# Two feature tiles of a feed-forward block by pairs of token tiles, with a new order of its first stage, on one Trainium2 core

## The chip, the cores and the metric

The kernel runs on one core of a Trainium2 chip. The metric is the device time of one execution in microseconds (us). Three runs of the kernel before took 2253.65, 2257.54 and 2258.06 us; the median is 2257.54 us. TensorE is the matmul engine (PE in the profile, PEld its weight loads), VectorE is DVE, ScalarE is ACT, GpSimd is POOL, and SyncE (SP) issues the DMAs. Each engine works through its own queue in order; an instruction that waits holds up what stands behind it on the same engine.

## The reference

Two layers of an encoder are applied to 512 prompt tokens and 256 sample tokens with the same weights (768 tokens, width 1024). A layer has four mixers side by side (grouped-query attention, differential attention, retention, RWKV-7) and then a gated feed-forward block of width 2816:

```python
mix = jnp.concatenate([o_a, o_b, o_c, o_d], axis=-1) @ p['w_out'][l]
x = x + _rms(mix, p['norm_mix_post'][l])
h = _rms(x, p['norm_ffn_pre'][l])
f = (jax.nn.silu(h @ p['ffn_w_gate'][l]) * (h @ p['ffn_w_up'][l])) @ p['ffn_w_down'][l]
x = x + _rms(f, p['norm_ffn_post'][l])
```

`_rms` scales a row by `rsqrt(mean(x*x) + eps)` and by a gain. All is float32.

## The kernel before

Each float32 operand of a matmul is split into a high part (a copy that ScalarE rounds) and a low part (the difference, by VectorE or GpSimd), and a product is three matmuls: high by high, high by low, low by high. The normalised activations stand transposed in `hh` and `hl`, eight rows of 128 features by 768 tokens; the tokens are six tiles of 128, tiles 0 to 3 of the prompt (sequence 0) and 4 and 5 of the sample (sequence 1).

The order of the instructions of the mixers, and of the start of the feed-forward block, is set by a planner that simulates the queues and gives earlier program text priority. Under `manual_schedule` the order is that of the program text. This holds from `ffn_head` (L1346) to the end of the block.

**The end of the mixers.** `out` (L1167) adds the last products, applies `post_norm` (L226) and `pre_norm` (L218) per token tile, and `split_T` (L201) transposes each normalised tile on TensorE (tile name `hT`) and writes `hh` and `hl`. Each norm calls `rsqrt` (L149): a tensor_scalar (multiply and add, L153, VectorE) and a power of -1/2 (L154, GpSimd). `rsqrt` is called at six places: two kinds of norm of whole rows (names `p`, `q`, and `q_`, `p_` at the block's end), the head norms of attention and retention (`ra`, `rb`, `rc`) and the group norm (`fr`).

**The feed-forward block.** The 22 feature tiles of 128 are worked off in order. Tiles 2 to 21 use a block product with seven instead of eight half-size products (`block_mm`, L1262, tile name `p`), which needs sums of blocks of the activations (`ffn_sums`, L1207) and of the weights (`w_sums`, L1325). The first two, f = 0 and f = 1, are plain products (`up_mm`, L1275, by `feat_mm`, L189; tile names `fg` for the gate and `fu` for the up weight): for each sequence, and for each pair of token tiles in it, 24 matmuls for `fg` and 24 for `fu`. While TensorE works on them, the other engines make the sums. `up_gate` (L1284) turns `fg` and `fu` into the gated activation: tanh (ScalarE, L1288), two products (VectorE, L1289 and L1290), the high part `ah` (ScalarE, L1291) and the low part `al` (VectorE, L1292).

The down products (`down_mm`, L1294, tile name `dn`) multiply the gated activations of two feature tiles by the down weights for one token tile and one half of the outputs: six matmuls each, twelve of them for f = 0 and 1. They use two PSUM banks in turn, and `down_add` (L1307) empties a bank: for this first group ScalarE copies it (L1310), for later ones VectorE adds it (L1312).

**The head, written by hand.** `ffn` (L1614) makes the products and the gate of f = 0 for sequence 0 under the planner. `ffn_head` then has, in this order: products of f = 0 for sequence 1; both parts of sums 0 (`next(sums[0])` twice: first the adds of L1218 and the differences L1219 and L1220 on GpSimd, then the differences L1228 and L1229 and the splits L1232 and L1233); the two splits of down weights; the gate of f = 0, sequence 1; sums 1, with the products of f = 1 for sequence 0 in the middle; the weight splits of f = 2 (`w_first`, `w_second`); both parts of sums 2; the gate of f = 1, sequence 0; the products of f = 1, sequence 1; the first part of sums 3; the weight sums of f = 2; the gate of f = 1, sequence 1; two down products; the second part of sums 3; four splits (`ffn_first`); two down products; `w_third`. The remaining eight down products stand in the units of f = 2 and f = 3 of `ffn_units` (L1390), four in each; later units have six.

PSUM has eight banks. The products of sequence 0 use the tag `pS` (two banks: one for `fg`, one for `fu`), those of sequence 1 the tag `pb` (two banks), the down products `pa` (two), and the transposes `pT` and `pO` (one each).

Of the kernel before, what the change touches and what calls it, by code (L numbers as in the profile page):

```python
# [14 lines left out]
ALU = mybir.AluOpType  # L15
# [11 lines left out]
NT = TOK // P  # L27
# [58 lines left out]
class Trunk:  # L86
# [62 lines left out]
    def rsqrt(self, src, n, scale, eps, name, tag):  # L149

        nc = self.nc
        r = self.tiny(tag, n, name, 4)
        nc.vector.tensor_scalar(out=r, in0=src, scalar1=scale, scalar2=eps, op0=ALU.mult, op1=ALU.add)  # L153
        nc.gpsimd.tensor_tensor(out=r, in0=r, in1=self.mhalf.to_broadcast([P, n]), op=ALU.pow)  # L154
        return r

# [1118 lines left out]
    def up_mm(self, l, f, s, wg, wu):  # L1275

        t0, n, *_r = SEQS[s]
        pg, pu = [self.bank(("pS", "pb")[s], f"{n}{l}_{f}_{s}") for n in ("fg", "fu")]
        for a in range(0, n, 256):
            self.feat_mm(pg[:, a:a + 256], *wg, P, t0 + a, 256)  # L1280
            self.feat_mm(pu[:, a:a + 256], *wu, P, t0 + a, 256)
        return pg, pu

    def up_gate(self, s, pg, pu, th, ah, al):  # L1284
        nc = self.nc
# [60 lines left out]
    def ffn_head(self, l, ws, tiles):  # L1346

        self.raw, self.w, self.tt, self.t1s = {}, {}, {}, []
        A, V = self.nc.gpsimd, self.nc.vector
        self.nbank = 0  # L1350
        sums = [self.ffn_sums(l, k) for k in range(4)]
        act = [t[1:] for t in tiles]
        self.rest = [(t, n) for n in range(2) for t in range(NT)]

        def down(n):
            for _i in range(n):
                t, half = self.rest.pop(0)
                self.down_add(*self.down_mm(l, 0, t, half, (act, self.w["d", 0, half])))

        self.down_load(l, 0, 0)  # L1360
        self.down_load(l, 0, 1)
        ps = self.up_mm(l, 0, 1, *ws[0])
        next(sums[0])
        next(sums[0])
        self.down_split(l, 0, 0, eng=V)
        self.w_load(l, 2, 0)
        self.down_split(l, 0, 1, eng=A)
        self.w_load(l, 2, 1)
        self.up_gate(1, *ps, *tiles[0])
        next(sums[1])  # L1370
        ps = self.up_mm(l, 1, 0, *ws[1])
        next(sums[1])
        self.w_first(l, 2, ("whi", "wlo"))
        self.w_second(l, 2)
        next(sums[2])
        next(sums[2])
        self.up_gate(0, *ps, *tiles[1])
        ps = self.up_mm(l, 1, 1, *ws[1])
        next(sums[3])
        self.w_sums(2)  # L1380
        self.up_gate(1, *ps, *tiles[1])
        down(2)
        next(sums[3])
        for k in range(4):
            self.ffn_first(k)
        down(2)
        self.w_third(l, 2)
        return act

    def ffn_units(self, l, act):  # L1390
# [3 lines left out]
        nc = self.nc  # L1394
# [5 lines left out]
        NG = NF // 2  # L1400
# [5 lines left out]
        for f in range(2, NF):  # L1406
            nxt = f + 1 if f + 1 < NF else None
            g, odd = f // 2, f % 2
            G, U = self.tmp(f"fg{l}_{f}"), self.tmp(f"fu{l}_{f}")
            c11, c12, c21, c22 = G[:, L], G[:, R], U[:, L], U[:, R]  # L1410
            downs = [] if g == NG - 1 else self.rest[4 * odd:4 * odd + 4] if g == 1 else [(t, odd) for t in range(NT)]

            def mm(n, key, j, h):
                return self.block_mm(f"p{n}{l}_{f}", w[f, key], j, h)
# [199 lines left out]
    def ffn(self, l):  # L1614
        if l + 1 < L:
            self.xd = [self.dr.tile([P, DM], F32, name=f"xd{l}_{t}") for t in range(NT)]

        tiles = [(self.tmp(f"th{l}_{f}"), self.slot("D", [P, TOK], f"ah{l}_{f}", F32R), self.slot("D", [P, TOK], f"al{l}_{f}", F32R)) for f in range(2)]
        ws = []
        for f in range(2):  # L1620
            ws.append([self.piece(l, PIECE_FF + 2 * f + i, tags=("Q", "Q") if f and i else ("whi", "wlo")) for i in range(2)])
            if f == 0:
                self.up_gate(0, *self.up_mm(l, 0, 0, *ws[0]), *tiles[0])
        with self.tc.manual_schedule():
            act = self.ffn_head(l, ws, tiles)
            self.late = self.ffn_end(l, self.ffn_units(l, act))
# [184 lines left out]
```

## Time and profile before

| what | value |
|---|---|
| median of three runs | 2257.54 us (2253.65 to 2258.06) |
| the profiled execution | 2247.12 us |
| its span, first to last instruction | 2245.3 us |
| granted TensorE clock, mean share of full speed | 0.984 |
| TensorE busy | 2111.9 us (94%) |
| VectorE busy | 1599.2 us (71%) |
| ScalarE busy | 917.5 us (41%) |
| GpSimd busy | 909.3 us (40%) |

The durations come from the profiled execution. Its span starts with the first and ends with the last instruction; 1.8 us of its time lie around the span. Its time is 10.4 us under the median of the runs. A row of the timeline has the start, the duration, the engine, the line, the operation, output and inputs, the shape and the count; in brackets stands the idle time of the engine before it and what ended that. Matmuls are pipelined, so the distance from start to start is what one costs TensorE, not its duration.

### The profile page before, as it was taken

The page shows a single profiled execution, that of the slowest core. Times are in us where ns is not written, and L with a number is a line of the kernel's source. Part 1 is how long each engine was busy: PE and PEld are TensorE (multiplying, and loading weights), DVE is VectorE, ACT ScalarE, POOL GpSimd, SP SyncE. Part 2 cuts the span into 40 slices and gives each one's busy share as a digit, 9 for nine tenths or more (in the row PEclk, how much of TensorE's full clock was granted, in tenths as well). Part 3 has the DMA queues.
Part 4 walks back from the last instruction along what each step waited for, and adds up shares of the span by engine and source line. Part 5 has one row for each costly group of instructions (what it writes and reads, how often), then busy time and mean ns, then how long its engine had stood idle before and what let it go on. Part 6 is the DMA issues. An engine that isn't in the chain of part 4 may idle for free.

```text
span 2245.3 us, 43651 instructions
## 1 busy us (share of the span) xinstructions
PE 2111.9 (94%) x17400; PEld 1923.2 (86%) x17400; DVE 1599.2 (71%) x2782; ACT 917.5 (41%) x1865; POOL 909.3 (40%) x733
## 2 busy tenths in 40 slices
PE   7989989989889999999999998899899899999998
PEld 7878878779879999999888898887788799999996
DVE  5597647885876767767766885588857676777665
ACT  4333325565534332333434333355654433232322
POOL 1342212334555445454523333133254545445454
PEclk9999989999999999999999999999999999999999
DMA  4544365344412221212425535733353112221223
GB/s 173 140 103 119 95 214 138 92 139 146 140 47 76 66 75 62 70 66 66 174 97 139 130 87 141 219 114 95 119 168 112 48 66 76 66 75 58 71 70 141
DMA packets 245099, 240.93 MB, mean 107 GB/s; under 512 B 138784, under 2 KB 191904, under 8 KB 244896
## 3 DMA queue, kind: packets, MB, share of 16 engines
q1 hardware_dynamic: 244896, 238.15, 34.8%
q8 instruction: 137, 2.24, 0.4%
q14 instruction: 66, 0.54, 0.1%
HBM read 183.03 MB, written 55.05 MB: 106 GB/s over the span
## 4 chain that ended last, share of the span: by engine, by line
PE 63%; DVE 17%; DMA 6%; POOL 4%; issue 4%; ACT 4%; SPq 1%; DVEq 0%; POOLq 0%; ACTq 0%
PE p L1271 23%; PE dn L1303 15%; PE dz L197 5%; DMA raw<-in_wp_dram 3%; PE op L186 3%; PE za L186 2%; PE zb L186 2%; DVE el L461 2%; DVE nper L463 2%; PE sd L174 1%; PE zv L186 1%; PE ob L174 1%; POOL wlo L168 1%; DVE wlo L168 1%; DVE xm L234 1%
## 5 line engine op out<-in xcount | busy, mean ns | idle before, releaser
L1259 POOL TENSOR_TENSOR wld<-raw,whd 128x1024 fp32r<-128x1024 f32 x42 | 108.6, 2585 | 360.2 <-ACT whd L1258 360.2
L1303 PE MATMUL dn<-whd,ah 128*128 128x512 f32 x528 | 210.9, 400 | 20.7 <-ACT ah L1291 18.0
L1303 PE MATMUL dn<-wld,ah 128*128 128x512 f32 x528 | 210.0, 398 | 1.5 <-POOL wld L1259 1.5
L1303 PE MATMUL dn<-whd,al 128*128 128x512 f32 x528 | 210.3, 398 | 0.0
L1312 DVE TENSOR_TENSOR y<-y,dn 128x512 f32<-128x512 f32 x216 | 147.3, 683 | 80.4 <-PE dn L1303 80.4
L168 POOL TENSOR_TENSOR wlo<-raw,whi 128x1024 fp32r<-128x1024 f32 (+1 forms) x46 | 108.4, 2356 | 181.0 <-ACT whi L165 163.6
L1271 PE MATMUL p<-ts,whb 128*128 128x384 f32 x560 | 144.7, 339 | 0.0
L1259 POOL TENSOR_TENSOR wla<-raw,wha 128x1024 fp32r<-128x1024 f32 x40 | 96.2, 2405 | 110.9 <-ACT wha L1258 110.9
L1398 DVE TENSOR_TENSOR fg<-fg,p 128x384 f32<-128x384 f32 x160 | 87.9, 549 | 63.0 <-PE p L1271 62.8
L1303 PEld LDWEIGHTS dn<-whd,ah 128*128 128x128 f32 x528 | 100.1, 190 | 37.3 <-ACT ah L1291 18.9
L1424 ACT ACTIVATE ft<-fg 128x384 f32<-128x384 f32 x80 | 42.0, 525 | 208.3 <-DVE fg L1398 208.3
L165 ACT ACTIVATE whi<-raw 128x1024 fp32r<-128x1024 f32 (+1 forms) x95 | 92.2, 971 | 83.9 <-DMA raw<-in_wp_dram 38.2
L1303 PEld LDWEIGHTS dn<-whd,al 128*128 128x128 f32 x528 | 99.9, 189 | 24.5 <-DVE al L1485 0.5
L1258 ACT ACTIVATE whb<-raw 128x1024 fp32r<-128x1024 f32 x40 | 42.5, 1062 | 189.8 <-POOL raw L1331 189.8
L1303 PEld LDWEIGHTS dn<-wld,ah 128*128 128x128 f32 x528 | 100.6, 191 | 17.8 <-POOL wld L1259 2.4
L186 PE MATMUL zc<-whi,hh 128*128 128x256 f32 x384 | 112.1, 294 | 2.7 <-ACT zc L794 2.3
L1428 DVE SCALAR_TENSOR_TENSOR fg<-ft,fg 128x384 f32<-128x384 f32 x80 | 85.6, 1070 | 40.4 <-ACT ft L1424 40.4
L186 PE MATMUL zc<-wlo,hh 128*128 128x256 f32 x384 | 109.8, 287 | 1.0 <-DVE wlo L168 1.0
L186 PE MATMUL zc<-whi,hl 128*128 128x256 f32 x384 | 109.6, 286 | 0.0
L1271 PEld LDWEIGHTS p<-ts,whb 128*128 128x128 f32 x560 | 102.5, 188 | 6.3
L1271 PE MATMUL p<-hl,whc 128*128 128x384 f32 x320 | 107.6, 336 | 0.0
L1271 PE MATMUL p<-hh,whc 128*128 128x384 f32 x320 | 107.5, 336 | 0.0
(463 smaller groups left out, 7201.7 us busy)
## 6 DMA issues: line engine op xcount, KB each, us to landing
raw<-in_wp_dram SPq DMA_DIRECT2D x184, 512.0 KB
raw<-in_wp_dram SPq DMA_DIRECT2D x38, 384.0 KB
kr<-kd SPq DMA_DIRECT2D x96, 64.0 KB
kr<-kd SPq DMA_DIRECT2D x48, 128.0 KB
x<-xm SPq DMA_DIRECT2D x24, 256.0 KB
xf<-x SPq DMA_DIRECT2D x12, 512.0 KB
gain<-in_bc_dram SPq DMA_DIRECT2D x8, 512.0 KB
bd<-sh SPq DMA_DIRECT2D x8, 512.0 KB
```

Source lines behind the costliest of these rows:

```text
L165: nc.scalar.activation(hi[:, :n], raw[:, :n], AF.Copy)
L168: eng.tensor_tensor(out=lo[:, :n], in0=raw[:, :n], in1=hi[:, :n].bitcast(F32), op=ALU.subtract)
L174: self.nc.tensor.matmul(ps[c], lhsT=lhsT[:, c], rhs=rhs, start=start, stop=stop)
L186: mm(ps, lhsT=a, rhs=b[:, c:c + ncol], start=i == 0, stop=i == tot - 1)
L197: mm(ps, lhsT=a, rhs=b, start=i == 0, stop=i == 3 * NK - 1)
L461: V.tensor_tensor(out=ev, in0=q[:, j + 1:32, j:j + 1].to_broadcast([96, m, j]), in1=q[:, j:j + 1, 0:j].to_broadcast([96, m, j]), op=ALU.mult)
L1259: eng.tensor_tensor(out=lo, in0=x, in1=hi.bitcast(F32), op=ALU.subtract)
L1271: self.nc.tensor.matmul(ps, lhsT=a, rhs=b, start=i == 0, stop=i == 11)
L1303: self.nc.tensor.matmul(ps, lhsT=a[p], rhs=b[q], start=i == 0, stop=i == 6 * len(pairs) - 1)
L1312: self.nc.vector.tensor_tensor(out=yt, in0=yt, in1=ps, op=ALU.add)
L1398: add = lambda o, x, y, op=ALU.add: V.tensor_tensor(out=o, in0=x, in1=y, op=op)
L1428: V.scalar_tensor_tensor(out=x, in0=th, scalar=1.0, in1=x, op0=ALU.add, op1=ALU.mult)
```

## The change

`rsqrt` runs its tensor_scalar on GpSimd. `up_mm` becomes a generator that yields after each pair of token tiles, and its banks go by feature tile (f = 0 has `pS`, f = 1 has `pb`) instead of by sequence. In `ffn`, both feature tiles make their products for token tiles 0 and 1 first, and then for tiles 2 and 3, each followed by its gate, all under the planner. In `ffn_head` the products of f = 1 for sequence 0 and their gate are gone, the weight splits of the down products stand before the second part of sums 0, gates, sums and weight splits have another order, and eight down products instead of four stand in the head, so that two instead of four are left for each of the units f = 2 and f = 3.

```diff
@@ rsqrt
-        nc.vector.tensor_scalar(out=r, in0=src, scalar1=scale, scalar2=eps, op0=ALU.mult, op1=ALU.add)
+        nc.gpsimd.tensor_scalar(out=r, in0=src, scalar1=scale, scalar2=eps, op0=ALU.mult, op1=ALU.add)
@@ up_mm
-        pg, pu = [self.bank(("pS", "pb")[s], f"{n}{l}_{f}_{s}") for n in ("fg", "fu")]
+        pg, pu = [self.bank(("pS", "pb")[f], f"{n}{l}_{f}_{s}") for n in ("fg", "fu")]
         for a in range(0, n, 256):
             self.feat_mm(pg[:, a:a + 256], *wg, P, t0 + a, 256)
             self.feat_mm(pu[:, a:a + 256], *wu, P, t0 + a, 256)
-        return pg, pu
+            yield pg, pu
@@ ffn_head
-        ps = self.up_mm(l, 0, 1, *ws[0])
-        next(sums[0])
+        ps = next(self.up_mm(l, 0, 1, *ws[0]))
         next(sums[0])
         self.down_split(l, 0, 0, eng=V)
         self.w_load(l, 2, 0)
         self.down_split(l, 0, 1, eng=A)
         self.w_load(l, 2, 1)
+        next(sums[0])
+        next(sums[1])
         self.up_gate(1, *ps, *tiles[0])
+        ps = next(self.up_mm(l, 1, 1, *ws[1]))
         next(sums[1])
-        ps = self.up_mm(l, 1, 0, *ws[1])
-        next(sums[1])
-        self.w_first(l, 2, ("whi", "wlo"))
         self.w_second(l, 2)
         next(sums[2])
+        self.w_first(l, 2, ("whi", "wlo"))
+        self.up_gate(1, *ps, *tiles[1])
+        down(2)
         next(sums[2])
-        self.up_gate(0, *ps, *tiles[1])
-        ps = self.up_mm(l, 1, 1, *ws[1])
+        down(2)
         next(sums[3])
         self.w_sums(2)
-        self.up_gate(1, *ps, *tiles[1])
         down(2)
         next(sums[3])
@@ ffn_units
-            downs = [] if g == NG - 1 else self.rest[4 * odd:4 * odd + 4] if g == 1 else [(t, odd) for t in range(NT)]
+            downs = [] if g == NG - 1 else self.rest[2 * odd:2 * odd + 2] if g == 1 else [(t, odd) for t in range(NT)]
@@ ffn
+        ups = []
         for f in range(2):
             ws.append([self.piece(l, PIECE_FF + 2 * f + i, tags=("Q", "Q") if f and i else ("whi", "wlo")) for i in range(2)])
-            if f == 0:
-                self.up_gate(0, *self.up_mm(l, 0, 0, *ws[0]), *tiles[0])
+            ups.append(self.up_mm(l, f, 0, *ws[f]))
+            next(ups[f])
+        for f in range(2):
+            self.up_gate(0, *next(ups[f]), *tiles[f])
```

## Rows read from the trace of the kernel before

**Rows 1.** Page, busy time (us), share of the span and instructions of each engine.
```profile
PE 2111.9 (94%) x17400; PEld 1923.2 (86%) x17400; DVE 1599.2 (71%) x2782; ACT 917.5 (41%) x1865; POOL 909.3 (40%) x733
```

**Rows 2.** Waits of TensorE: us in total, times, longest us.
```profile
PE dn L1303 <- ACT ah L1291: 18.0, 2, 9.0
...
PE fg L197 <- DVE hl L211: 2.7, 4, 1.1
PE hT L206 <- DVE hl L211: 2.6, 2, 2.4
```

**Rows 3.** Timeline of TensorE in the first layer's head.
```profile
627.52 0.27 PE L197 MATMUL fu<-hh,wlo 128*128 128x256 f32 x1
627.64 0.28 PE L197 MATMUL fg<-hh,whi 128*128 128x256 f32 x1
...
633.34 0.40 PE L1303 MATMUL dn<-whd,ah 128*128 128x512 f32 x1
...
633.81 0.40 PE L1303 MATMUL dn<-whd,al 128*128 128x512 f32 x1
643.25 0.80 PE L1303 MATMUL dn<-whd,ah 128*128 128x512 f32 x1 [9.05 <-ACT ah L1291]
```

**Rows 4.** Timeline of ScalarE in the same head.
```profile
638.17 1.53 ACT L1232 ACTIVATE ts<-t 128x384 fp32r<-128x384 f32 x3 [8.30 <-DVE t L1228]
639.61 0.58 ACT L1288 ACTIVATE th<-fg 128x512 f32<-128x512 f32 x1
642.57 0.63 ACT L1291 ACTIVATE ah<-th 128x512 fp32r<-128x512 f32 x1 [2.38 <-DVE th L1290]
...
646.08 0.58 ACT L1310 ACTIVATE y<-dn 128x512 f32<-128x512 f32 x1
```

**Rows 5.** Timeline of VectorE in the same head.
```profile
629.57 3.23 DVE L1218 TENSOR_TENSOR t<-hh,hl 128x384 f32<-128x384 f32 x2
636.81 1.33 DVE L1228 TENSOR_TENSOR t<-t,t 128x384 f32<-128x384 f32 x1 [4.00 <-POOL t L1220]
...
643.84 1.02 DVE L1218 TENSOR_TENSOR t<-hh,hl 128x384 f32<-128x384 f32 x2
```

**Rows 6.** Timeline of GpSimd in the same head.
```profile
629.95 2.44 POOL L1259 TENSOR_TENSOR wla<-raw,wha 128x1024 fp32r<-128x1024 f32 x1 [3.70 <-ACT wha L1258]
...
635.78 0.99 POOL L1220 TENSOR_TENSOR t<-t,t 128x384 f32<-128x384 f32 x1
```

**Rows 7.** The chain that ended last, two pieces: start us, us, what.
```profile
643.25 7.77 PE dn L1303 x21
...
1755.24 6.59 PE dn L1303 x21
```

**Rows 8.** Stretches: us, then busy us of PE, PEld, DVE, ACT, POOL, clock, DMA share, GB/s.
```profile
580.00:611.00 31.00, 26.98 (x208) 25.58 (x207) 29.55 (x40) 16.12 (x28) 15.37 (x12) 0.94 0.37 121
611.00:634.00 23.00, 23.00 (x192) 22.72 (x191) 17.77 (x23) 6.98 (x12) 14.30 (x11) 1.00 0.15 47
```

**Rows 9.** Timeline of TensorE before the second layer's head.
```profile
1708.57 0.66 PE L206 MATMUL hT<-cs,xn 128*128 128x128 f32 x4 [2.40 <-DVE hl L211]
...
1711.31 0.58 PE L197 MATMUL fg<-hl,whi 128*128 128x256 f32 x1 [1.12 <-DVE hl L211]
```

**Rows 10.** First layer, second weight split of f = 4, and the product that reads it.
```profile
690.50 1.27 DVE L1259 TENSOR_TENSOR wlb<-raw,whb 128x1024 fp32r<-128x1024 f32 x1
...
699.11 0.52 PE L1271 MATMUL p<-ts,whb 128*128 128x384 f32 x2
```

**Rows 11.** Lines L153 and L154: duration ns min/median/max, first and last start us, forms.
```profile
L153 DVE TENSOR_SCALAR p5r<-p x3: 145/151/154, 11.1 to 1713.1; 128x1 f32<-128x1 f32 x3
...
L154 POOL TENSOR_TENSOR p5r<-p5r,mhalf x3: 548/549/553, 11.4 to 1713.4; 128x1 f32<-128x1 f32 x3
```

**Rows 12.** Groups of GpSimd by form: busy us, mean ns, idle before and its releaser.
```profile
L168 POOL TENSOR_TENSOR wlo<-raw,whi 128x1024 fp32r<-128x1024 f32 x26 | 68.7, 2644 | 136.2 <-ACT whi L165 118.8 <-PE sb L987 9.6 <-DMA nper<-nb 7.8
...
L553 POOL MEMSET br<- 64x128 f32 x96 | 19.1, 199 | 102.6 <-issue 31.0 <-ACT pb L756 24.9 <-ACT vb L794 10.7
```

## The prediction

> **What bounds the kernel now.** I read the busy times of the engines first: TensorE is busy for 94% of the span, so it sets the pace, and only what leaves it idle or slow can be won [rows 1]. The list of TensorE's waits says where: the longest single entry is the down product in the two heads of the feed-forward block, 18.0 us in two waits for `ah` [rows 2]. The timeline shows one of them. The products of f = 1 for sequence 0 are done at 627.6 and those for sequence 1 at 633.3; three matmuls of the first down product then run, and the fourth waits 9.05 us, until 643.25 [rows 3]. Its input was ready on TensorE's side 15 us earlier, but ScalarE starts its tanh only at 639.61, behind three splits of sums 2, which waited 8.30 us [rows 4]. VectorE, ahead of those, waited 4.00 us for GpSimd's difference L1220 [rows 5], and GpSimd was late because its weight split had first waited 3.70 us [rows 6]. So the gate stands in the queues behind sums that it doesn't need. After the wait TensorE is slow too: the chain has 21 down matmuls in 7.77 us in the first layer and 6.59 in the second [rows 7], where two steps take 0.47 us at full speed [rows 3], so 21 take 4.94.
>
> The stage before is another matter: from 580 to 611 VectorE is busy for 29.55 of 31 us [rows 8]. TensorE's smaller waits there (2.7 and 2.6 us over both layers [rows 2], most of them in the second [rows 9]) are for the norms of the token tiles.
>
> **The change part by part.**
>
> *The gate of f = 1, sequence 0, leaves the queue behind sums 2.* This removes the two waits, 18.0 us [rows 2]. It should also remove the slow matmuls behind them, 7.77 + 6.59 - 2 x 4.94 = 4.5 us [rows 3, 7].
>
> *What is late next.* The head now has eight down products. The third needs a bank that ScalarE must empty, and this copy (0.58 us [rows 4]) stands in ScalarE's queue behind `ah` of the last gate, and so behind VectorE. VectorE was busy 17.77 us from 611 to 634 with what still comes before that point [rows 8]; to this comes the gate of f = 1, sequence 0, about 2 us, and the last gate's two products, about 1 us (estimates from the step of the same width on ScalarE, 0.63 [rows 4], and half of it). That is 611 + 21 = 632, and with 3 to 5 us of hand-offs to ScalarE and waits for GpSimd the `ah` is done near 636 and the first copy near 637. TensorE's plain products end near 632 in the first layer (below), two down products of 6 x 0.235 = 1.41 us follow until 635, and the third waits about 2 us. The copies of the next two stand behind the three splits of sums 2 (1.53 us [rows 4]), which is another wait of about 2.3. In the second layer TensorE arrives some 3 us earlier, so its first wait is longer. I take 4.3 + 7.0 = 11.3 us for both layers. The bounds are nothing (the copies in time) and 18.0 + 4.5, the wait of now; I stand in the middle because the same three engines hand over as often as before.
>
> *The products by pairs of token tiles.* The 48 matmuls of f = 1 for tiles 0 and 1, 48 x 0.12 = 5.76 us by the step between two rows [rows 3], move ahead of tiles 2 to 5 and can fill TensorE's waits for their norms. No work is added. In the second layer the waits that they can fill are 2.40 + 1.12 us [rows 9] and about 1.1 in smaller ones, 4.6. In the first, the fourth weight is split too late for the longest wait, and 1.4 are left. I take 6.0; the bounds are 0 (the planner puts them behind the norms' transposes, or in front of them, where they delay VectorE's stage by what they fill) and 11.5 (both times in full). The new banks cost nothing: f = 0 of sequence 1 needs the first gate done, and 5.76 us of products of f = 1 cover its two VectorE products; without that cover it would wait about 2 us per layer.
>
> *Fewer down products in f = 2 and f = 3.* The same work is done, 4 x 1.41 = 5.6 us per layer earlier, so nothing is added. What covers the shorter units is that their weights are early: the split `wlb` of f = 4 ends at 691.8 and is read at 699.11 [rows 10], 7.3 us of slack, against units that get shorter by 2.8 us each. If that cover were gone, 5.6 us per layer would come back.
>
> *The weight splits of the down products earlier, and their loads.* `w_load` follows each split on SP's queue and so goes out earlier by the second part of sums 0. Nothing but these loads stands behind them there. Cost nothing; without this the weight split of f = 2 on GpSimd would wait as it does now, 3.70 us [rows 6].
>
> *The tensor_scalar of `rsqrt` on GpSimd.* It takes 0.15 us on VectorE [rows 11]. No row shows it on GpSimd: a memset of 64x128 takes 0.20 and the power of one column 0.55 [rows 11, 12]; I take 0.3, nearer to the memset, since the power is the heavier function. A hand-over from VectorE to GpSimd goes away, and VectorE, full in the stage of the norms, is spared eight of them, 1.2 us per layer. At the very end of the kernel the step is on the path and costs between a gain of 0.1 and a loss of 0.4. I put the sum at 0, between -2 and +2. The Trainium skill (GPSIMD Engine Reference, Elementwise — side-by-side cycle accounting) has GpSimd about half as fast as VectorE at an add. By this the step would take 0.30 us and the sum would be the same.
>
> **The sum**: 18.0 + 4.5 - 11.3 + 6.0 + 0 = 17.2 us less. The profiled execution took 2247.1 us, so it would take 2229.9. The runs shown have a median 10.4 us higher; on that scale the forecast is 2240 us.
>
> **The rivals.**
>
> *The gate in front of the sums (2250 us, chance 0.14).* The planner may put the gate of f = 1, sequence 0, in VectorE's queue ahead of sums 0. Its products end near 618, VectorE would stand from 612 until then, and GpSimd behind it. Sums, weight sums and copies come 6 us later, and of 17.2 some 12 are lost over both layers minus the wait for the copies that falls together with it, which leaves about 8. For it: the gate stands earlier in the text. Against it: the planner goes by what is ready: in the trace a weight load of the head goes out on SP's queue ahead of the last norms' stores, which stand earlier in the text.
>
> *The weights late in f = 2 and f = 3 (2251 us, 0.06).* If the chain of loads and sums cannot follow, 2 x 5.6 = 11.2 us come back and 6 are left. The 7.3 us of slack speak against it [rows 10].
>
> *VectorE and GpSimd hold each other up (2251 us, 0.07).* VectorE's two adds of sums 2 take 3.23 us beside GpSimd's work, and those of sums 3, where GpSimd mostly waits, 1.02 [rows 5]. If the new order packs the two engines so tightly that each VectorE step of the head is stretched like that, the copies come later by 5 us per layer, and 7 of the 17 are left. The Trainium skill (SBUF — State Buffer, SBUF: two separate sides) says that GpSimd and a VectorE operation with two SBUF inputs exclude each other for a whole instruction. The trace agrees in kind. Against: the sum of the work is unchanged, and GpSimd had idle time in its queue.
>
> *Slower: the mixers planned anew (2268 us, 0.13).* `rsqrt` is also used 46 times inside the mixers, under the planner. On GpSimd the tensor_scalar stands behind weight splits of 2.64 us [rows 12] that it did not have to wait for. If half of the 46 wait for one such split and half of those reach TensorE, this costs 46 / 4 x 2.64 = 30 us, which is 13 more than the gain. It decides from 22 us on, 8 or 9 such sites. For it: a planner's order can shift over a whole layer. Against: the power behind it was in the same queue already.
>
> **How the numbers follow.** A measurement of this kernel tells about 0.2%, 4.5 us, from no change. The forecast has 0.60, the rivals 0.14, 0.06, 0.07 and 0.13. Of the first I count all as faster, of the next three most (0.15) as faster and 0.12 as the same, and of the last nearly all as slower: faster 0.75, same 0.12, slower 0.13. The lowest end is the case without new waits: 18.0 + 4.5 + 6.0 + 2 = 30.5, 2227. The upper end takes in the three weak gains and half the spread of the runs, 2255. The likeliest case alone has 2228 to 2249.
>
> **What the profile would show.** If right, the 9 us wait of `dn` for `ah` is gone from the list; two shorter waits of `dn` stand in each head, ended by ScalarE's copies L1310 or the `ah` of the last gate; products of f = 1 stand between the transposes of the last token tiles; f = 2 starts its first block product with eight down products done. The steps fail where the head has one wait over 8 us, where `p` waits for `whb`, or where the stretches of the mixers differ from before by more than 5 us; a longer mixer would make the forecast wrong.

## The result and the profile after

The changed kernel takes 2267.5 us (median of 7 runs, 2262.3 to 2270.4) beside 2254.5 us for the kernel before in the same rounds (7 runs, 2246.2 to 2258.1). The ratio of after to before is 1.0056, 95% interval 1.0041 to 1.0071: 12.6 us slower. The forecast was 2240 us, with a range of 2227 to 2255 us. The profiled execution took 2270.4 us. On the page TensorE is as busy as before [rows 1], VectorE has 94 instructions fewer and GpSimd 94 more:

```profile
PE 2124.8 (94%) x17400; PEld 1936.4 (85%) x17400; DVE 1602.8 (71%) x2688; ACT 917.0 (40%) x1865; POOL 936.0 (41%) x827
```

The waits of TensorE (us in total, times, longest): the 18.0 us of [rows 2] are gone, and waits for ScalarE's copies have come, the longest again 9.0 us. Both rows are new.

```profile
PE dn L1303 <- ACT y L1310: 20.9, 6, 9.0
...
PE dn L1303 <- ACT ah L1509: 5.3, 2, 2.7
```

In the first layer's head TensorE (timeline: start us, us, what, idle before and what ended it) starts its down products 4.8 us earlier than in [rows 3] and stands just as long, two products later:

```profile
628.51 0.40 PE L1303 MATMUL dn<-whd,ah 128*128 128x512 f32 x1
...
640.42 0.79 PE L1303 MATMUL dn<-whd,ah 128*128 128x512 f32 x1 [8.95 <-ACT y L1310]
...
651.80 0.34 PE L1271 MATMUL p<-hh,whr 128*128 128x384 f32 x1
```

VectorE shows why. Before, the adds of sums 0 (L1218) started at 612.01:

```profile
612.01 1.84 DVE L1218 TENSOR_TENSOR t<-hh,hl 128x384 f32<-128x384 f32 x2
```

After, the gate of f = 1, sequence 0, stands ahead of sums 0, and VectorE waits 1.43 and 1.52 us for products that are only then computed. The adds of sums 0 run at 619.24. The last gate's two products start at 638.50, behind a weight split (wlr) that takes 2.83 us beside GpSimd's split:

```profile
615.04 0.69 DVE L1289 SCALAR_TENSOR_TENSOR th<-th,fg 128x512 f32<-128x512 f32 x1 [1.43 <-ACT th L1288]
617.24 0.69 DVE L1290 SCALAR_TENSOR_TENSOR th<-th,fu 128x512 f32<-128x512 f32 x1 [1.52 <-PE fu L197]
...
619.24 1.02 DVE L1218 TENSOR_TENSOR t<-hh,hl 128x384 f32<-128x384 f32 x2
...
635.75 2.83 DVE L1259 TENSOR_TENSOR wlr<-raw,whr 128x512 fp32r<-128x512 f32 x1
638.50 0.41 DVE L1289 SCALAR_TENSOR_TENSOR th<-th,fg 128x256 f32<-128x256 f32 x1
```

ScalarE's copy, the releaser of the 8.95 us, follows its `ah` of the last gate at once; forecast for it was 637:

```profile
639.47 0.42 ACT L1291 ACTIVATE ah<-th 128x256 fp32r<-128x256 f32 x1 [3.48 <-DVE th L1290]
639.79 1.06 ACT L1310 ACTIVATE y<-dn 128x512 f32<-128x512 f32 x2
```

Where the time went shows best by stages, from the first gate product to the last down product of a layer (feed-forward) and what lies between (mixers). Rows of stretches (us; busy us of PE, PEld, DVE, ACT, POOL; clock; DMA share; GB/s), two executions of each kernel, the second from the runs c1 and c2. Before: the two feed-forward stages and, between them in time, the mixers of layer 1:

```profile
588.51:1136.53 548.02, 528.57 (x2828) 487.45 (x2827) 400.67 (x518) 195.52 (x286) 272.30 (x166) 0.99 0.24 80
1136.53:1697.03 560.50, 524.74 (x5866) 469.74 (x5864) 402.35 (x863) 260.84 (x644) 184.31 (x199) 0.98 0.46 133
1697.03:2238.03 541.00, 525.18 (x2804) 486.06 (x2804) 379.71 (x495) 183.30 (x267) 266.58 (x162) 0.99 0.22 75
```

Before, second execution (c1), the mixers:

```profile
1136.61:1709.10 572.49, 535.43 (x5865) 478.50 (x5864) 405.60 (x864) 263.68 (x647) 180.78 (x200) 0.96 0.46 131
```

After, the same three:

```profile
589.33:1139.12 549.79, 529.20 (x2828) 487.82 (x2827) 400.32 (x505) 195.12 (x285) 278.29 (x179) 0.98 0.24 80
1139.12:1718.77 579.65, 532.73 (x5866) 478.97 (x5865) 402.00 (x829) 260.55 (x644) 192.18 (x233) 0.96 0.45 128
1718.77:2261.06 542.29, 525.28 (x2806) 485.36 (x2804) 386.34 (x486) 182.74 (x266) 268.91 (x171) 0.99 0.22 75
```

The feed-forward stages repeat: both layers together 1089.0 and 1088.0 before, 1092.1 and 1092.0 after. So the part of the kernel that the change was made for is 3.5 us longer. The mixers do not repeat. Two executions of the kernel before, with one and the same order of instructions, differ by 12 us in layer 1, of which 10.7 are TensorE's busy time at a lower clock; the second execution of the changed kernel had 572.35 there. A mixer stage of one trace says little; the rest of the 12.6 us, about 9, is told by medians alone. By these traces it lies in the mixers of layer 1: up to the first gate product of layer 0 the two traces of before take 588.5 and 587.4 us and those of after 589.3 and 587.4, and behind the last down product all four take 7.3 to 7.5.

Inside the feed-forward stage, starts in us after its first gate product, layer 0 / layer 1, from the first rows of each piece:

| | before | c1 | after | c2 | e4 |
|---|---|---|---|---|---|
| first down product | 44.8 / 48.4 | 45.0 / 44.1 | 39.2 / 40.5 | 39.2 / 40.5 | 42.2 / 41.7 |
| f = 2 | 62.4 / 64.6 | 62.5 / 61.0 | 62.5 / 63.8 | 62.5 / 63.8 | 60.8 / 60.3 |
| f = 4 | 102.9 / 105.2 | 103.1 / 101.6 | 98.1 / 99.4 | 98.2 / 99.5 | 96.4 / 96.0 |
| f = 5 | 126.0 / 128.3 | 126.2 / 124.7 | 127.1 / 128.3 | 127.2 / 128.4 | 125.3 / 125.1 |

After has eight down products behind it where f = 2 starts, before four (1.41 us each); where f = 5 starts the work done is the same. The changed kernel is 4.8 us ahead where f = 4 starts in layer 0, and 1.1 us behind where it ends.

That unit holds the second of the new waits. TensorE before and after, layer 0 (start of f = 2, start of f = 4, the first matmul of f = 4 that reads the `ah` of f = 3, start of f = 5):

```profile
650.86 0.34 PE L1271 MATMUL p<-hh,whr 128*128 128x384 f32 x1
...
691.45 0.33 PE L1271 MATMUL p<-hh,whr 128*128 128x384 f32 x1
...
698.41 0.39 PE L1303 MATMUL dn<-whd,ah 128*128 128x512 f32 x1
...
714.53 0.34 PE L1271 MATMUL p<-hh,whr 128*128 128x384 f32 x1
```

```profile
687.47 0.33 PE L1271 MATMUL p<-hh,whr 128*128 128x384 f32 x1
...
697.26 0.50 PE L1303 MATMUL dn<-whd,ah 128*128 128x512 f32 x1 [2.67 <-ACT ah L1509]
...
716.45 0.34 PE L1271 MATMUL p<-hh,whr 128*128 128x384 f32 x1
```

The same unit as a stretch, from the start of f = 4 to that of f = 5, before and after (columns as above). Of the 5.9 us more, 3.5 are idle time of TensorE and 2.4 are busy time, at a granted clock of 0.94 instead of 1.00:

```profile
691.45:714.53 23.08, 23.08 (x121) 21.46 (x121) 16.88 (x22) 7.80 (x11) 10.71 (x6) 1.00 0.26 90
```

```profile
687.47:716.45 28.98, 25.43 (x121) 22.77 (x121) 21.53 (x27) 9.24 (x13) 15.96 (x10) 0.94 0.20 66
```

And ScalarE's `ah` of f = 2 and f = 3, before and after:

```profile
673.75 0.85 ACT L1509 ACTIVATE ah<-fg 128x768 fp32r<-128x768 f32 x1 [1.22 <-DVE fg L1431]
...
694.13 0.85 ACT L1509 ACTIVATE ah<-fg 128x768 fp32r<-128x768 f32 x1 [1.28 <-DVE fg L1431]
```

```profile
676.16 0.85 ACT L1509 ACTIVATE ah<-fg 128x768 fp32r<-128x768 f32 x1 [1.22 <-DVE fg L1431]
...
696.37 0.84 ACT L1509 ACTIVATE ah<-fg 128x768 fp32r<-128x768 f32 x1 [1.22 <-DVE fg L1431]
```

From `ah` to `ah` are 20.4 us before and 20.2 after. TensorE's unit with four down products took 20.3 us before ((691.45 - 650.86) / 2), the same; this alone doesn't tell which of the two sets the pace, since each waits for the other. The changed kernel does: TensorE goes through f = 2 and f = 3 in 17.8 us each ((687.47 - 651.80) / 2), and `ah` still takes 20.2. So this is the pace of the other engines, which go round from the weight load over GpSimd's split and sums to `wlb`, the gate and the next split `wlc`. The load of the second weight of f = 4 goes out as `wlc` of f = 3 ends, and its split `wha` starts 3.6 us after that end before and 3.5 after, where it waits for the load; so the loop had next to no slack before either (VectorE and ScalarE, before, then after):

```profile
676.07 1.23 DVE L1259 TENSOR_TENSOR wlc<-raw,whc 128x1024 fp32r<-128x1024 f32 x1 [0.47 <-ACT whc L1258]
680.94 1.05 ACT L1258 ACTIVATE wha<-raw 128x1024 fp32r<-128x1024 f32 x1
```

```profile
678.47 1.23 DVE L1259 TENSOR_TENSOR wlc<-raw,whc 128x1024 fp32r<-128x1024 f32 x1 [0.48 <-ACT whc L1258]
683.24 1.06 ACT L1258 ACTIVATE wha<-raw 128x1024 fp32r<-128x1024 f32 x1 [1.66 <-DMA raw<-in_wp_dram]
```

With two down products less, TensorE's unit runs into the `ah` of f = 3, which is itself 2.2 us later (1.4 counted from the first gate product), since the sums of the head were late.

### The profile page after: what moved, and what is told of

Same layout as the page of the kernel before. It is cut to its first block, busy times and chain, and to the rows that moved or that the text cites. A ratio compares the mean times of both kernels' runs of the same rounds, so it can differ in the third digit from the quotient of the medians.

```text
span 2268.5 us, 43640 instructions
## 1 busy us (share of the span) xinstructions
PE 2124.8 (94%) x17400; PEld 1936.4 (85%) x17400; DVE 1602.8 (71%) x2688; ACT 917.0 (40%) x1865; POOL 936.0 (41%) x827
## 4 chain that ended last, share of the span: by engine, by line
PE 59%; DVE 18%; DMA 7%; POOL 7%; ACT 4%; issue 4%; SPq 2%; DVEq 0%; POOLq 0%; ACTq 0%
PE p L1271 20%; PE dn L1303 12%; PE dz L197 5%; PE op L186 3%; PE zb L186 3%; DMA raw<-in_wp_dram 2%; PE zc L186 2%; DVE el L461 2%; PE za L186 2%; DVE nper L463 1%; PE sd L174 1%; POOL yg L1541 1%; POOL wla L1259 1%; DVE wlo L168 1%; PE fu L197 1%
## 5 line engine op out<-in xcount | busy, mean ns | idle before, releaser
L1312 DVE TENSOR_TENSOR y<-y,dn 128x512 f32<-128x512 f32 x216 | 146.9, 682 | 80.5 <-PE dn L1303 80.5
L1303 PEld LDWEIGHTS dn<-wld,ah 128*128 128x128 f32 x528 | 101.0, 191 | 17.8 <-POOL wld L1259 2.1
```

Of the source, the lines that this page charges most:

```text
L1303: self.nc.tensor.matmul(ps, lhsT=a[p], rhs=b[q], start=i == 0, stop=i == 6 * len(pairs) - 1)
L1312: self.nc.vector.tensor_tensor(out=yt, in0=yt, in1=ps, op=ALU.add)
```

## The experiments

Theory A: the step of `rsqrt` on GpSimd makes the mixers longer. Theory B: the gate that the planner put in front of sums 0 makes the wait of 8.95 us. The first four kernels cross the two.

**e1**, the kernel before with that step alone:

```diff
-        nc.vector.tensor_scalar(out=r, in0=src, ...
+        nc.gpsimd.tensor_scalar(out=r, in0=src, ...
```

> The kernel before with nothing but the tensor_scalar of rsqrt moved to GpSimd. Theory A (the moved step alone makes the mixers of the second layer longer, which came to 16.5 us between the first dz matmul and the last transpose): this kernel is 12 to 20 us slower than before, near 2267 us on a scale where before takes 2254, with its mixers of layer 1 longer by over 10 us. Rival A2 (the mixers were lengthened by another edit, such as the generator in up_mm or the new place of the head): within 3 us of before. Rival A3 (the mixers' plan shifts with any edit, by chance): a change of either sign of 3 to 15 us, in the first layer as well as in the second.

Measured 0.9999 of before (0.9986 to 1.0011). The move costs nothing on the kernel before, though both mixers are planned anew. A falls in its plain form; the time is where A2 has it.

**e2**, the changed kernel with the step back on VectorE (the same line reversed).

> The changed kernel with the tensor_scalar of rsqrt back on VectorE. Theory A: 15 to 20 us faster than the changed kernel, so near 2250, about 4 us faster than before, since the head's part of the change is worth about 3 us in the first layer and about as much in the second. Rival A2: within 3 us of the changed kernel, 2267. If the heads keep their wait of 8.95 us for the copies L1310, the order of the gate has nothing to do with rsqrt's engine.

1.0025 (1.0009 to 1.0040): 5.6 us slower than before, 7 us faster than the changed kernel, between what A and A2 had. Here the instructions of the mixers stand in the order of before on every engine, and the feed-forward stages, 1095.4 us, are 6.9 us longer. So the edits of the feed-forward block by themselves cost the whole 5.6 us. The wait of 8.96 us is there too, so the order of the gate doesn't hang on the engine of `rsqrt`.

**e3**, the changed kernel with the gate by hand behind sums 0:

```diff
         self.w_load(l, 2, 1)
         next(sums[0])
+        self.up_gate(0, *ps10, *tiles[1])
         next(sums[1])
...
-            self.up_gate(0, *next(ups[f]), *tiles[f])
+            ps = next(ups[f])
+            if f == 0:
+                self.up_gate(0, *ps, *tiles[0])
...
```

> The changed kernel with the gate of f = 1, sequence 0, put by hand behind both parts of sums 0. Theory B (this gate, which the planner put in front of sums 0 on VectorE, makes VectorE and GpSimd about 7 us late and is the cause of the wait of 8.95 us of the third down product): that wait shrinks to 2 to 4 us, and the kernel is 8 to 13 us faster than the changed kernel. Rival B2 (the copies are late because of the last gate and the weight split in front of it, whatever the first gate's place): the wait stays over 7 us and the time within 3 us.

**e4**, both.

> The changed kernel with both: the gate of f = 1, sequence 0, behind sums 0 and the tensor_scalar of rsqrt on VectorE. If theories A and B hold side by side the gains add: 25 to 32 us faster than the changed kernel, near 2238 us, which is 13 to 18 us faster than before. If A2 holds: 8 to 13 faster than the changed kernel only; if B2 holds: 15 to 20.

e3 1.0048 (1.0030 to 1.0066), e4 0.9986 (0.9973 to 0.9998). On the head B holds in both, for half of the wait: 4.29 us are left in e3 and 4.28 in e4, a little more than the 2 to 4 expected. The feed-forward stages are 1082.7 us in e3 (9.4 less than after; 8.0 for the same work, since 12 matmuls of the mixers, about 1.4 us at 0.12 each, lie in the stage of layer 1 in after and ahead of it in e3) and 1084.6 in e4 (10.8 less than e2). The lines of e4:

```profile
624.49 0.39 PE L197 MATMUL fg<-hh,whi 128*128 128x256 f32 x1 [1.62 <-DVE th L1289]
...
637.54 0.57 PE L1303 MATMUL dn<-whd,ah 128*128 128x512 f32 x1 [4.28 <-ACT y L1310]
...
694.32 0.50 PE L1303 MATMUL dn<-whd,ah 128*128 128x512 f32 x1 [2.67 <-ACT ah L1510]
```

The gate's later place costs a wait of 1.62 us: the products of f = 1, sequence 1, need the banks that it empties. In e3 the gain doesn't reach the total, which is 2 us under that of the changed kernel and not 8 to 13: its mixers of layer 1, planned anew once more, stand 15 us over before (table below). e4 is 16 us faster than the changed kernel, not 25 to 32. That is where A without B was expected, but e1 speaks against A and the halved wait against B2. It is the only kernel of this study whose interval lies under that of before, by 3 us; that is less than the 0.2% that counts as a change here.

Two theories on what is left. D: the pace of VectorE, GpSimd and ScalarE bounds the start of the block, and what TensorE wins in front of it is lost again. E: each wait of TensorE counts for itself. Three edits on e4 follow. **e5**:

```diff
-        self.w_first(l, 2, ("whi", "wlo"))
         self.up_gate(1, *ps, *tiles[1])
+        self.w_first(l, 2, ("whi", "wlo"))
```

> The kernel e4 (gate behind sums 0, rsqrt on VectorE) with the weight split of w_first for f = 2 put behind the last gate of the head; the order of both mixers is that of e4. In e4 the third down product waited 4.28 us for the copy, and the last gate's VectorE work stood behind this split of 2.84 us. Theory D (what bounds the start of the feed-forward block is not TensorE but the chain of splits and sums on VectorE, GpSimd and ScalarE, which ends in the ah of f = 3; the down product of f = 4 waits for it, and what TensorE wins in front of it is lost there): the wait in the head shrinks to 1 to 2 us, the wait of the down product of f = 4 grows from 2.67 to 4 to 6 us, and the time stays within 2.5 us of e4. Rival E (each wait of TensorE counts for itself): 5 to 7 us faster than e4.

**e6**:

```diff
             p = mm(4, "a", 0, 4)
-            down()
+            down(f != 4)
...
             p = mm(5, "c", 0, 1)
-            down()
+            down(2 if f == 4 else 1)
```

> The kernel e4 with the first down product of f = 4 moved one block product later, nothing else; the planner plans the mixers of layer 1 otherwise than in e4, which may be worth some us of either sign. Theory D: the first down product of f = 4 no longer waits over 1 us (it starts 2.1 us later, the ah of f = 3 was 2.67 late), 3 to 4.5 us per layer are won, and the kernel is 6 to 9 us faster than e4 but for the mixers; the feed-forward stages of the trace, from the first gate product to the last down product, are shorter by that. Rival E2 (the block products of f = 4 then wait for their own weights): the wait moves to p for whb or whc, and nothing is won.

**e7**, both:

> Both edits on e4: the split of w_first behind the last gate, the first down product of f = 4 one block product later; mixers planned as in e6. Theory D: with the wait of f = 4 out of the way part of what the head wins counts, so 0 to 3 us faster than e6, the rest appearing as a wait of the down product of f = 4 again. Rival E: 5 to 7 us faster than e6.

e5 1.0005 (0.9992 to 1.0018), no less than the 0.9986 of e4, and the feed-forward stages 3 us longer: nothing is won, E falls. But the wait came back 8 us later, at the next copies, and not at f = 4 as D had it; and the time is 4 us over e4, not within 2.5. D is right only in that nothing is won. The next copies stand on ScalarE behind the splits of sums 2, for which VectorE waits 3.06 us for GpSimd, and GpSimd has no idle time from 636.5 to 645:

```profile
639.45 0.50 PE L1303 MATMUL dn<-whd,ah 128*128 128x512 f32 x1 [2.04 <-ACT y L1310]
...
647.49 0.79 PE L1303 MATMUL dn<-whd,ah 128*128 128x512 f32 x1 [4.97 <-ACT y L1310]
...
698.50 0.50 PE L1303 MATMUL dn<-whd,ah 128*128 128x512 f32 x1 [1.22 <-ACT ah L1510]
```

e6 1.0041 (1.0026 to 1.0057) and e7 1.0053 (1.0037 to 1.0068), both a miss: slower than e4 by 12 and 15 us, the stages by 11 and 9. In e6 the wait for `ah` fell from 2.67 to 0.41 us as expected, and one of 5.45 us for a bank came, which VectorE's sum L1312 empties, behind `wlr`, for which VectorE had waited 2.61 us:

```profile
696.62 0.50 PE L1303 MATMUL dn<-whd,ah 128*128 128x512 f32 x1 [0.41 <-ACT ah L1510]
...
710.58 0.79 PE L1303 MATMUL dn<-whd,ah 128*128 128x512 f32 x1 [5.45 <-DVE y L1312]
```

**e8** keeps the banks as in e4 and gives f = 4 a first down product that needs no `ah` of f = 3:

```diff
-            downs = [] if g == NG - 1 else self.rest[2 * odd:2 * odd + 2] if g == 1 else [(t, odd) for t in range(NT)]
+            if g == 1:
+                downs = [(0, *x) for x in (self.rest[2:3] if odd else self.rest[:2])]
+            elif g == 2:
+                downs = [(1, t, 0) for t in range(5, 6)] + [(1, t, 1) for t in range(NT)] if odd else [(0, *self.rest[3])] + [(1, t, 0) for t in range(5)]
+            else:
+                downs = [] if g == NG - 1 else [(g - 1, t, odd) for t in range(NT)]
...
-                        t, half = downs.pop(0)
-                        due.append(self.down_mm(l, g - 1, t, half, (acts[g - 1], w["d", g - 1, half])))
+                        k, t, half = downs.pop(0)
+                        due.append(self.down_mm(l, k, t, half, (acts[k], w["d", k, half])))
```

> The kernel e4 with one of the down products of group 0 taken from f = 3 and put first in f = 4, so that the first down product that needs the ah of f = 3 comes one block product (2.1 us) later, while the products in flight and their two banks stay as in e4 (in e6 the wait moved to a bank, 5.5 us for y of L1312). Theory D: the wait of 2.67 us for the ah of f = 3 falls under 1 us, no wait of over 2 us takes its place before f = 6, and the feed-forward stages are 2.5 to 4.5 us shorter than e4's in each layer (547.2 and 537.5 us there); the time 5 to 9 us under e4 but for what the mixers of layer 1, planned anew, add or take. Rival G (the chain of VectorE, GpSimd and ScalarE bounds f = 4 in more than one place, so each wait that is taken away comes back at the next): the stages within 2 us of e4's.

1.0012 (0.9992 to 1.0031), stages 1089.4 us against 1084.6 in e4. The wait for `ah` is gone and four others of over 0.5 us stand within 30 us, for the weights, for a copy (0.71 us) and for sums:

```profile
684.51 0.44 PE L1271 MATMUL p<-hh,whr 128*128 128x384 f32 x1 [1.09 <-ACT whr L1258]
...
709.29 0.49 PE L1303 MATMUL dn<-whd,ah 128*128 128x512 f32 x1 [2.10 <-DVE y L1312]
...
712.87 0.79 PE L1303 MATMUL dn<-whd,ah 128*128 128x512 f32 x1 [1.25 <-DVE y L1312]
```

Rival G holds in kind, as the other engines bound these units in more than one place; but the stages are 4.8 us longer than e4's, where G had them within 2. **e9** moves in f = 3 also `w_third` behind the sum and the tanh.

> As e8, and in f = 3 the weight split wlb for f = 4 put behind the last sum and the tanh of f = 3, so that these no longer stand behind it on VectorE and ScalarE. Theory D: the ah of f = 3 comes 1 us or more earlier against the gate of the head than in e4 and nothing waits for it; 0 to 1 us per layer less than e8 in the feed-forward stages. Rival G: p of f = 4 waits for whb or wlb instead, and the stages are as long as e4's or longer.

1.0007 (0.9991 to 1.0024), stages 1091.9 us: longer than e4's, as rival G has it, but no product waits for `whb` or `wlb`. The waits stand at `whr` (1.00 us) and at the banks that the sums L1312 empty (2.08 and 1.70).

**c1** and **c2** are the two kernels unchanged.

> The kernel before, unchanged, for a second trace. The first trace was of an execution 10 us under the median. Theory F (the difference between executions of the same order lies in the mixers, in how often the clock falls behind their small waits): the two feed-forward stages agree with the first trace within 2 us each, and the mixers of layer 1, 560.5 us there, are longer by 5 to 12 us. Rival: the difference is spread over all stages in proportion.

> The changed kernel, unchanged, for a second trace. By theory F (differences between executions of one order lie in the mixers) the feed-forward stages agree with the first trace, 549.8 and 542.3 us, within 2 us, and the mixers of layer 1, 579.6 us there, come out between 570 and 585: longer than the 560.3 and 572.5 us of the two traces of before.

c1: 549.2 and 538.8 us in the feed-forward stages, mixers of layer 1 12 us longer: theory F in the main, though the stage of layer 1 differs by 2.2 us, a little more than the 2 that F allows (up to the first down product it is 4.3 us, 48.4 and 44.1 in the table above; some of that is made up behind it). c2: 549.6 and 542.4, and 572.35 us in the mixers of layer 1, no longer than c1's. The first traces alone would have put 19 us there.

**e10** and **e11** divide the step of `rsqrt` by its callers on the changed kernel:

```diff
-        nc.gpsimd.tensor_scalar(out=r, in0=src, ...
+        (nc.gpsimd if tag == "sr" else nc.vector).tensor_scalar(out=r, in0=src, ...
```

> The changed kernel with only the norms of whole rows (p and q, 128x1) on GpSimd and those of the mixers' heads (ra, rb, rc, fr) back on VectorE. TensorE's order in the mixers of layer 1 is then that of before and of e2 again, but for the last stage with the rows' norms. Theory H (the loss between e2 and the changed kernel, 1.0025 to 1.0056, comes with the new plan of the mixers of layer 1, which the head norms' place on GpSimd brings about): 0 to 2.5 us over e2, near 1.003 of before. Rival J (the rows' norms beside full GpSimd and VectorE, 0.5 to 0.75 us each in place of 0.15, are what costs): 5 to 8 us over e2, near 1.0055 of before.

> The reverse: only the mixers' head norms on GpSimd. The mixers of layer 1 are planned anew. Theory H: 4 to 9 us over e2, near 1.0055 of before, with the mixers of layer 1 longer than 575 us in the trace. Rival J: 0 to 2.5 us over e2. If neither e10 nor this kernel is over e2 by more than 2.5 us, the cost is the luck of one plan and belongs to no instruction (as e1 says already, where the same move cost nothing).

e10 0.9996 (0.9982 to 1.0009), e11 (with `!=`) 1.0016 (1.0000 to 1.0031). Neither is slower than e2, so no group of these instructions carries the 7 us. That e10 is even under e2, whose head it shares, lies at the edge of the two intervals.

All kernels in one table: time against before from the ratio (of 2255 us), the part of it in the feed-forward stages (their sum less 1088.5, the mean of before and c1), and what remains for the mixers and the ends.

| kernel | total | feed-forward | rest |
|---|---|---|---|
| after | +12.6 | +3.5 | +9.1 |
| e1 before, rsqrt moved | -0.2 | -1.3 | +1.1 |
| e2 after, rsqrt back | +5.6 | +6.9 | -1.3 |
| e10 rsqrt moved for rows | -0.9 | +4.2 | -5.1 |
| e11 rsqrt moved in mixers | +3.6 | +5.2 | -1.6 |
| e3 gate later | +10.8 | -4.4 | +15.2 |
| e4 gate later, rsqrt back | -3.2 | -3.9 | +0.7 |
| e5 on e4 | +1.1 | -0.9 | +2.0 |
| e6 on e4 | +9.2 | +7.1 | +2.1 |
| e7 on e4 | +12.0 | +5.5 | +6.5 |
| e8 on e4 | +2.7 | +2.3 | +0.4 |
| e9 on e4 | +1.6 | +3.4 | -1.8 |

In e3, e8 and e10 the planner puts 12 matmuls of the mixers on the other side of a stage's start; their middle column is corrected by 1.4 us for that. The totals are known to about 3 us, and the middle column, from one trace of most kernels, to 1 or 2. It follows the edits of the block: with the changed head +3.5 to +6.9 where the planner sets the gate, about -4 with its later place (e3, e4). The last column follows no edit: the full move of `rsqrt` stands at +1, +9 and +15.

## Why the prediction was wrong

*The products by pairs* were forecast at 6.0 us, with 11.5 as the end. In the changed kernel the first down product comes 5.6 us earlier in layer 0, and 5.8 in layer 1 by the mean of the two traces of before. The stretch from the first gate product to it, layer 0, in before, after and e2 (columns as above):

```profile
588.51:633.34 44.83, 40.81 (x322) 39.41 (x321) 39.15 (x51) 17.62 (x30) 26.61 (x20) 0.96 0.24 82
```

```profile
589.33:628.51 39.18, 38.06 (x323) 37.88 (x321) 30.51 (x37) 15.05 (x25) 23.48 (x21) 1.00 0.27 92
```

```profile
586.81:630.54 43.73, 40.55 (x322) 40.38 (x321) 33.23 (x41) 15.75 (x28) 22.50 (x18) 0.92 0.25 85
```

The mechanism was right: TensorE's idle time falls from 4.0 to 1.1 us. But half of the gain is one that I had not in the term: the same matmuls take 2.8 us less, at a granted clock of 1.00 instead of 0.96. And the term can't be called too small, since part of the gain came together with the move of `rsqrt`: in e2, without that move, the first down product comes 1.1 us earlier than before in layer 0 and 5.4 in layer 1, 6.5 in all and near the forecast. There the longest wait, for the norm of token tile 4, is 3.18 us and the clock 0.92; with one trace of e2 it is open how much of this is the engine of `rsqrt` and how much the execution.

*"What is late next"* is the first step that failed. The sum had 22.5 us going and 11.3 coming. From the first down product to f = 2, less 1.41 us for each down product, the head took 11.9 us before in layer 0 and 12.0 after; in layer 1 10.6 and 11.3 in the two traces of before, and 12.0 after. Nothing went: the wait of 9.05 us for `ah` [rows 3] became one of 8.95 us for the copy, which the forecast had at about 2. The rival that the planner puts the gate ahead of sums 0 came true, and its price was not 8 us of 17 but all of this term. I set its chance at 0.14 by a weight load that had gone ahead in SP's queue; the order of VectorE's own instructions was the evidence that was wanted. e3 and e4 show the place of the gate to be the cause of most of it: with the gate behind sums 0 the same measure is 7.3 or 7.4 us in each layer of both kernels, 8 us less than before over both layers, of the 11.2 forecast; the wait of 1.5 or 1.6 us per layer for the banks goes off that. What also came, the weight split of 2.83 us in front of the last gate, is no loss by itself: e5 takes it away, on e4, and wins nothing. The rival of VectorE and GpSimd holding each other up did not come true: from the first gate product to f = 2, layer 0, VectorE was busy 51.7 us before and 49.6 after.

*"Fewer down products in f = 2 and f = 3: cost nothing"* is the second. I read the cover off `wlb` and the product that reads it, 7.3 us [rows 10]. But `ah` of f = 3 stands in VectorE's and ScalarE's queues behind that split, and the down product that reads it had 3.4 us: 698.41 against 694.13 + 0.85. From f = 2 to f = 5 the units take 64.6 us in both layers with 10 down products, and took 63.7 with 14: 1.0 + 5.6 = 6.6 us per layer are lost, 13.2 in all. This was the rival "weights late", at 0.06 and with 11.2 us, in another queue than I had looked in. e6, e8 and e9 show that moving this wait only moves it. No run gives the units their down products back and leaves the rest of the change, so the 6.6 us are read from traces, of before and after twice each, and not from an experiment on this edit alone.

*`rsqrt` at 0* was right for the step: it costs nothing in e1. What stands beside it is +9 us in the mixers of the changed kernel, which e2, with the mixers in the order of before, doesn't have. That this is the plan, and not the step, is argued from e1, e10 and e11, where the same instructions move and cost nothing or less; the rival of new plans had it as a slower step behind weight splits, which they don't bear out. Why one plan is longer than another is still open.

Together: -11.4 by the pairs, +1.2 in the head and +13.2 in the units make +3.0, near the 3.5 us measured in these stages, and 9.1 more come from the rest. Against a sum of -17.2 the first two failed steps took 12.4 and 13.2 us, the plan 9.1, and the pairs gave 5.4 back. The time came out at the 2268 us of the slower rival by chance, as three rivals came true at once. I had given them chances as if only one could come true; they share no condition, and their prices add. Of my signs of failing, the wait of over 8 us in the head came (8.95), the wait for `whb` did not, and the mixers' 5 us say little, since two traces of the kernel before differ by 12.

## What to carry to other kernels

Before you take work away from the engine that sets the pace, follow the loop that feeds it from one output to the next (here 20.4 us against 20.3) and see where in it there is time to spare; where there is none, as between `wlc` and `wha` here, little is to be had from a shorter unit. Equal distances alone don't show it. Read slack at the last reader in the queue, not at the first. And where a planner orders the rest of the program, an edit's price is that of a new plan too (here up to 15 us beside a step that costs nothing by itself), so the stage that the edit was made for has to be judged by its own stretch, with a second trace of either kernel.

## What was unexpected on the chip

The same program, in the same order, spends 560.5 or 572.5 us in one stage. The rows above show its clock at 0.98 and 0.96 and 10.7 us more of busy TensorE for the same matmuls; the feed-forward stages agree within 2.2 us.

The step of `rsqrt` on GpSimd takes 0.19 us in most places and 0.51 to 0.75, by the medians, in several of the crowded norms of whole rows (line L153 after: duration ns min/median/max):

```profile
L153 POOL TENSOR_SCALAR rc<-ssc x16: 191/192/398, 168.1 to 1395.6; 128x4 f32<-128x4 f32 x8, 128x2 f32<-128x2 f32 x8
...
L153 POOL TENSOR_SCALAR p4r<-p x3: 191/750/753, 5.6 to 1731.4; 128x1 f32<-128x1 f32 x3
```

I had taken 0.3. On VectorE it was 0.15 [rows 11], so 0.19 is 1.3 times as long. The Trainium skill (GPSIMD Engine Reference, Elementwise — side-by-side cycle accounting) has 1.96 times for an add of 2048 elements; for so small a step the measurement decides.

VectorE and GpSimd held each other up. Where GpSimd stands idle, the split `wlr` (128x512) takes 0.69 us (before, VectorE; GpSimd's next step is at 629.95 [rows 6]):

```profile
628.97 0.69 DVE L1259 TENSOR_TENSOR wlr<-raw,whr 128x512 fp32r<-128x512 f32 x1
```

In e4 it takes 2.84 us in the head and 0.98 in the unit f = 3, and each time it ends 0.54 or 0.55 us after GpSimd's `wla` (timelines of the two engines):

```profile
632.85 2.84 DVE L1259 TENSOR_TENSOR wlr<-raw,whr 128x512 fp32r<-128x512 f32 x1
...
683.41 0.98 DVE L1259 TENSOR_TENSOR wlr<-raw,whr 128x512 fp32r<-128x512 f32 x1 [3.21 <-ACT whr L1258]
```

```profile
632.38 2.77 POOL L1259 TENSOR_TENSOR wla<-raw,wha 128x1024 fp32r<-128x1024 f32 x1 [3.95 <-ACT wha L1258]
...
681.44 2.40 POOL L1259 TENSOR_TENSOR wla<-raw,wha 128x1024 fp32r<-128x1024 f32 x1 [2.12 <-ACT wha L1258]
```

The Trainium skill (SBUF — State Buffer, SBUF: two separate sides) says that such an operation and one of GpSimd exclude each other for a whole instruction. The trace agrees: some 0.6 us are the split's own work, and the rest of the 2.84, about 2.2 us by estimate from these rows, is waiting that counts as busy.
